# Four elementwise sums of a Conformer encoder's feed-forward blocks moved from VectorE to GpSimd

## The chip, the cores and the metric

The kernel runs on one core of one Trainium2 chip, as one launch. The metric is the device time of one execution in microseconds (us); lower is better. Engines are called by their names or by the profile's short forms: TensorE (PE, with PEld for its weight loads), VectorE (DVE), ScalarE (ACT), GpSimd (POOL) and SyncE (SP), which issues most loads. DMA issues on GpSimd's queue are done by GpSimd itself.

## The reference

Two layers of a Conformer-like block on 512 tokens of 1024 features, in float32:

```python
def swiglu(x, w_gate, w_up, w_down):
    return (jax.nn.silu(x @ w_gate) * (x @ w_up)) @ w_down

for l in range(DEPTH):                       # DEPTH = 2
    x = x + 0.5 * swiglu(rms_norm(x, ffn1_norm[l]), ffn1_w_gate[l], ffn1_w_up[l], ffn1_w_down[l])
    h = rms_norm(x, mix_norm[l])
    p = h @ w_in[l]
    attn = mla_group(...)                    # latent attention, 8 heads
    conv = conv_group(...)                   # gated depthwise convolution
    x = x + jnp.concatenate([attn, conv], axis=-1) @ w_out[l]
    x = x + 0.5 * swiglu(rms_norm(x, ffn2_norm[l]), ffn2_w_gate[l], ffn2_w_up[l], ffn2_w_down[l])
    x = rms_norm(x, post_norm[l])
```

The weights of a feed-forward block are 1024 x 2816 (gate and up) and 2816 x 1024 (down). There are four such blocks, and the change is in these alone.

## The kernel before

**Precision.** Each float32 operand is split into a rounded high part and a low part (operand minus high part), and a product is three matmuls: high x high (L154), high x low (L155), low x high (L156). ScalarE makes the high part of weights (`wh`, L244), VectorE the low part (`wl`, L246, in `split_into`). Where a weight needs no sum, the low part comes from a copy with the sign turned (L389) onto which GpSimd's DMA queue adds the weights from memory (L390, in `subtracted` and `summed`).

**Fewer products.** Most of the feed-forward work uses a Winograd form of Strassen's scheme: a 2 x 2 block product is made with seven block products instead of eight, at the price of sums of the inputs and of the outputs. `pair` makes two of the 22 column blocks of gate and up, from four quarters of the weights, `a11`, `a12`, `a21` and `a22`, which SyncE loads. VectorE makes four sums of these: `s3` (L408), `a21` (L409), `a11` (L410) and last `a12` (L411), each of 128 x 1024. The seven products are, in TensorE's order, `b11` and `b21` (plain quarters), `t2` (weight `a11` after L410), `t3` (weight `s3`), `t1` (weight `a21`), `t4` (plain `a22`) and `b22` (weight `a12` after L411). So the sum of L411 is read only by the last product. Products with 512 columns at a time run through `product_joined` (L373 and L374). Their results are copied or added out of PSUM (L414 to L440), with the activation silu between.

**Output sums.** Of the eleven pairs in a block, the first two are computed plainly, six form two chunks of three, and the last three are plain on the down side. In the six, the results `s` and `s2` of a pair become operands of a down product in the same seven-product form. Their sums are `u` (L449 and L450) and `v` (L451 and L452), each of two halves of 128 x 256. `u` serves the products `t3` and `t2`, `v` the products `t1` and `t4`. `split` (L161 on ScalarE, L162 on VectorE) makes high and low parts of each.

**Down products.** After three pairs, `down` runs twice (two halves of the output columns, `g` 0 and 1) over four weight quarters of 128 x 768, with sums `s3` (L489), `a21` (L491), `a11` (L492) and `a12` (L496). The products are added to `x` (L480, which reads PSUM).

**Order.** A scheduler that simulates a timeline puts each engine's instructions in a fixed order; each engine then works its queue in that order. `after("first")` and the like (`issue_after`) tell it to put instructions behind a named one; this binds only instructions on the named one's own engine. The names here, `"first"`, `"second"`, `"u"` and `"v"`, are all VectorE instructions. Buffers come from pools of a fixed number (four for `fr`, three for `raw`, two for `ls`), so a load can start when the last reader of the old content is done.

**GpSimd elsewhere.** In the feed-forward blocks GpSimd issues the DMAs of L390 and little else. In the mixer stage and around it, it does elementwise work: L144 (low weights of the output projection), L191 (sums of squares), L930 (the convolution) and L173 (powers).

Of the kernel before, what the change touches and what calls it, by code (L numbers as in the profile page):

```python
# [12 lines left out]
ALU = mybir.AluOpType  # L13
# [61 lines left out]
def encoder_kernel(ctx: ExitStack, tc: tile.TileContext, xT, consts, vecs, rgain, wgu1, wd1, wdq1,  # L75
# [21 lines left out]
    def bank():  # L97
        return psum.tile([P, S], FP, tag="ps", name=nm("ps"))
# [4 lines left out]
    V, A, G, T = nc.vector, nc.scalar, nc.gpsimd, nc.tensor  # L103
# [149 lines left out]
    def ffn_body(fpool, l, gx, norm, wgu, wd, wdq, gain, done, w0, halved):  # L253
# [15 lines left out]
        def quarters(w, n, first=False):  # L269

            a = quarter(), quarter() if first else late(), quarter(), quarter()
            for q in range(4):
                nc.sync.dma_start(out=a[q][:, :n], in_=w[q])
            return *a, late()
# [81 lines left out]
        def product(o, w, n, start, stop):  # L356
            with tc.issue_after(order["pe"]):
                for gu in range(2):
                    for k in range(4):
                        hi, lo = X[n][k // 2]  # L360
                        t = slice(k % 2 * HS, (k % 2 + 1) * HS)
                        c = slice(gu * 512 + k * P, gu * 512 + (k + 1) * P)
                        last = mm3(o[:, gu * HS:(gu + 1) * HS], w[0][:, c], w[1][:, c], hi[:, t], lo[:, t],
                                   start and gu == 0 and k == 0, stop and k == 3, True)
            order["pe"] = last
# [16 lines left out]
        def copied(o, src):  # L382
            A.copy(o, src)
            return o
# [15 lines left out]
        def pair(p, quartered):  # L400

            a11, a12, a21, a22, s3 = quarters(wgu[l, p], WC, p == CHUNKS[0][1])
            bx, by, bz = bank(), (bank(), bank()), (bank(), bank())
            product(bx, split_into("a11", a11), "b11", True, True)
            a = copied(tmp(), bx)
            product_joined(by, summed(wgu[l, p, 1], a12), "b21", True)
            with after("first"):
                V.tensor_tensor(s3, a11, a21, ALU.add)  # L408
                V.tensor_tensor(a21, a21, a22, ALU.add)  # L409
                V.tensor_tensor(a11, a11, a21, ALU.add)  # L410
                V.tensor_tensor(a12, a12, a11, ALU.add)  # L411
            s = tmp()
            for c, main, rest in parts(by):
                V.tensor_tensor(a[:, c], a[:, c], main, ALU.add)  # L414
                V.tensor_tensor(a[:, c], a[:, c], rest, ALU.add)
                if c.start == 0:
                    A.activation(s[:, 0:HS], a[:, 0:HS], AF.Silu)
            V.tensor_tensor(s[:, 0:HS], s[:, 0:HS], a[:, HS:S], ALU.mult)
            product(bx, split_into("s2", a11), "t2", False, True)
            r2 = wide(fpool.tile([P, WC], FP, tag="e", name=nm("e"), bufs=1))  # L420
            copied(r2[:, 0], bx)
            product_joined(bz, split_into("s3", s3), "t3", True)
            d = tmp()
            for c, main, rest in parts(bz):
                A.copy(d[:, c], main)
                V.tensor_tensor(d[:, c], d[:, c], rest, ALU.add)  # L426
            product(bx, split_into("s1", a21), "t1", False, True)
            copied(r2[:, 1], bx)
            order["first"] = V.tensor_tensor(r2[:, 1], d, r2[:, 1], ALU.subtract).ins
            product_joined(bz, summed(wgu[l, p, 3], a22), "t4", False)  # L430
            for c, main, rest in parts(bz):
                V.tensor_tensor(r2[:, 0, c], main, r2[:, 0, c], ALU.subtract)
                V.tensor_tensor(r2[:, 0, c], rest, r2[:, 0, c], ALU.add)  # L433
            s2 = tmp()
            s2v = s2.rearrange("p (h t) -> p h t", h=2)
            A.activation(s2v, r2[:, :, 0:HS], AF.Silu)
            V.tensor_tensor(s2v, s2v, r2[:, :, HS:S], ALU.mult)
            product(bx, split_into("s4", a12), "b22", False, True)
            A.activation(s[:, HS:S], bx[:, 0:HS], AF.Silu)
            V.tensor_tensor(s[:, HS:S], s[:, HS:S], bx[:, HS:S], ALU.mult)  # L440
            if not quartered:
                return [split(s), split(s2)]
            h0, h1 = slice(0, HS), slice(HS, S)
            b = slot(FR)
            A.copy(b[:, h0], s[:, h0])
            V.tensor_tensor(b[:, h1], s[:, h0], b[:, h0].bitcast(FP), ALU.subtract)
            b2 = split(s2)
            u, v = fpool.tile([P, S], FP, tag="u", name=nm("u"), bufs=1), tmp()
            V.tensor_tensor(u[:, h0], s[:, h1], s2[:, h1], ALU.subtract)  # L449
            order["u0"] = V.tensor_tensor(u[:, h1], u[:, h0], s[:, h0], ALU.subtract).ins  # L450
            V.tensor_tensor(v[:, h0], s[:, h0], s[:, h1], ALU.subtract)  # L451
            V.tensor_tensor(v[:, h1], s2[:, h0], u[:, h1], ALU.add)  # L452
            us = split(u)
            order["u"] = order["evicted"]
            vs = split(v)
            order["v"], order["vh"] = order["evicted"], order["high"]
            return [{"b11": (b[:, h0], b[:, h1]), "b21": [w[:, h0] for w in b2], "b22": [w[:, h1] for w in b2],
                     "t3": [w[:, h0] for w in us], "t2": [w[:, h1] for w in us],
                     "t1": [w[:, h0] for w in vs], "t4": [w[:, h1] for w in vs]}]

        def down(act, chunk):

            n = 2 * NP * P
            for g in range(2):
                a11, a12, a21, a22, s3 = quarters(wdq[l, g, chunk], n)
                px, py, pz = bank(), bank(), bank()

                def times(o, src, name, start, q=None, lo=None):
                    hi, lo = split_into(name, src, n) if q is None else summed(wdq[l, g, chunk, q], src, n, lo)
                    with tc.issue_after(order["pe"]):  # L470
                        for k in range(NP):
                            for i in range(2):
                                c = slice((i * NP + k) * P, (i * NP + k + 1) * P)
                                last = mm3(o[:, i * HS:(i + 1) * HS], hi[:, c], lo[:, c], *act[k][name],
                                           start and k == 0 and i == 0, k == NP - 1, True)
                    order["pe"] = last

                def add(row, h, o, sign):
                    v = x[:, 4 * g + 2 * (1 - row):4 * g + 2 * (1 - row) + 2, h * HS:(h + 1) * HS]
                    return V.scalar_tensor_tensor(v, o.rearrange("p (m t) -> p m t", m=2), 0.5 * sign, v, ALU.mult,  # L480
                                                  ALU.add).ins
                times(px, a11, "b11", True)
                with after("u0"):
                    add(0, 0, px, 1)
                times(py, a12, "b21", True, 1)
                with after("u"):
                    add(0, 0, py, 1)
                with after("first") if g else nullcontext():
                    V.tensor_tensor(s3[:, :n], a11[:, :n], a21[:, :n], ALU.add)  # L489
                with after("first"):  # L490
                    V.tensor_tensor(a21[:, :n], a21[:, :n], a22[:, :n], ALU.add)  # L491
                    V.tensor_tensor(a11[:, :n], a11[:, :n], a21[:, :n], ALU.add)  # L492
                times(px, a11, "t2", False)
                order["second"] = add(1, 0, px, -1)
                with after("second" if g == 0 else "first"):
                    V.tensor_tensor(a12[:, :n], a12[:, :n], a11[:, :n], ALU.add)  # L496
                lo = subtracted(wdq[l, g, chunk, 3], a22, n)
                with after("u"):
                    times(pz, s3, "t3", True)
                add(1, 1, pz, 1)  # L500
                with after("v"), after("vh"):
                    times(px, a21, "t1", False)
                    order["first"] = add(1, 1, px, -1)
                    times(pz, a22, "t4", False, 3, lo)
                    add(1, 0, pz, 1)
                with after("v"), after("vh"):
                    times(px, a12, "b22", False)
                add(0, 1, px, 1)
# [732 lines left out]
```

## Time and profile before

| | us |
|---|---|
| median of 3 runs | 1804.17 |
| lowest and highest | 1803.3, 1804.97 |
| the profiled execution, its own time | 1804.94 |
| its span, first to last instruction | 1803.1 |

The page of the profile, in part: busy time of each engine (share of the span, count of instructions), the span in 40 slices (a digit is the busy share in tenths), and DMA.

```
DVE  7898988689956989898779989876998668989884
ACT  5565656457953575756645656554779435656564
POOL 1000010258943000000310000002689410000102
PEclk9999999999999999999999999999999999999999
```

The stretches where POOL has a digit of 2 or more are the mixer stages and the ends of blocks; the rows of 0 and 1 are the feed-forward blocks. A row of the timeline has the start in us from the span's start, the duration in us, engine, line, operation, tiles written and read, sizes, and in brackets the engine's idle time before it and what ended that. Records of one engine can overlap a little, since the next instruction starts while the last one drains.

### The profile page before, as it was taken

What the parts mean: (1) busy time and instruction counts of PE and PEld (TensorE: products, weight loads), DVE (VectorE), ACT (ScalarE), POOL (GpSimd) and SP (SyncE); (2) the same over time, 40 slices, a digit from 0 to 9 for tenths busy, and PEclk for the clock granted to TensorE, in tenths of its full rate; (3) what the DMA queues carried; (4) which work ended last, traced back from release to release, by engine and by line L of the source; (5) the groups of instructions that cost most, each with busy time, mean ns of one, the idle gap of its engine ahead of it and who ended that gap; (6) DMA issues with size and microseconds to landing.
All of it is one profiled execution on the core that took longest, in us unless ns stands there. A gap on an engine that the chain in (4) does not pass through costs nothing. (4 is left out here: it accounts for less than half of the span.)

```text
span 1803.1 us, 29267 instructions
## 1 busy us (share of the span) xinstructions
PE 1781.6 (99%) x11334; PEld 1603.1 (89%) x11334; DVE 1493.0 (83%) x2263; ACT 1091.9 (61%) x1721; POOL 420.2 (23%) x343
## 2 busy tenths in 40 slices
PE   9999999999999999999999999999999999999998
PEld 7899999888788899999888999998978788999997
DVE  7898988689956989898779989876998668989884
ACT  5565656457953575756645656554779435656564
POOL 1000010258943000000310000002689410000102
PEclk9999999999999999999999999999999999999999
DMA  5657574325103466665426575743250125575742
GB/s 167 173 127 182 134 174 125 108 88 136 29 24 100 124 167 160 153 159 129 125 63 169 126 191 122 193 110 111 80 151 3 42 83 161 139 183 134 180 119 74
DMA packets 70412, 226.16 MB, mean 125 GB/s; under 512 B 7936, under 2 KB 8320, under 8 KB 70272
## 3 DMA queue, kind: packets, MB, share of 16 engines
q1 hardware_dynamic: 54000, 169.74, 29.7%
q0 software_dynamic: 16128, 54.53, 17.6%
q8 instruction: 89, 1.46, 0.3%
q14 instruction: 51, 0.42, 0.1%
q10 hardware_dynamic: 144, 0.00, 0.0%
HBM read 222.15 MB, written 2.10 MB: 124 GB/s over the span
## 5 line engine op out<-in xcount | busy, mean ns | idle before, releaser
L155 PE MATMUL ps<-r,wh 128*128 128x256 f32 (+1 forms) x2540 | 805.8, 318 | 0.0
L154 PE MATMUL ps<-r,wh 128*128 128x256 f32 (+1 forms) x2540 | 802.9, 320 | 2.3 <-ACT wh L1060 1.5
L156 PE MATMUL ps<-r,wl 128*128 128x256 f32 (+1 forms) x2348 | 750.0, 321 | 1.7 <-DVE wl L246 1.6
L154 PEld LDWEIGHTS ps<-r,wh 128*128 128x128 f32 x2540 | 480.4, 189 | 44.1 <-ACT wh L138 3.7
L155 PEld LDWEIGHTS ps<-r,wh 128*128 128x128 f32 x2540 | 481.4, 190 | 34.2 <-issue 1.4
L156 PEld LDWEIGHTS ps<-r,wl 128*128 128x128 f32 x2348 | 445.0, 190 | 36.7 <-DVE wl L246 3.2
L373 PE MATMUL ps<-xj,wh 128*128 128x512 f32 x864 | 304.8, 392 | 4.6 <-DVE t L426 4.6
L138 ACT CAST wh<-raw 128x1024 fp32r<-128x1024 f32 (+3 forms) x148 | 132.3, 903 | 203.6 <-PE ps L155 100.3
L390 POOL DMA_DIRECT2D ls<-in_wgu x72 | 62.5, 869 | 734.4 <-ACT ls L389 656.5
L244 ACT CAST wh<-fr 128x1024 fp32r<-128x1024 f32 (+1 forms) x160 | 157.8, 986 | 109.7 <-DVE fr L410 51.3
L144 DVE TENSOR_TENSOR wl<-raw,wh 128x1024 fp32r<-128x1024 f32 (+3 forms) x132 | 145.2, 1108 | 84.7 <-ACT wh L138 84.3
L246 DVE TENSOR_TENSOR wl<-fr,wh 128x1024 fp32r<-128x1024 f32 (+1 forms) x160 | 182.1, 1138 | 20.5 <-ACT wh L244 20.5
L373 PEld LDWEIGHTS ps<-xj,wh 128*128 128x128 f32 x864 | 161.3, 188 | 36.3 <-DVE t L426 6.2
L930 POOL TENSOR_TENSOR y<-y,pr 128x511 f32<-128x511 f32 (+14 forms) x120 | 158.1, 1318 | 54.9 <-ACT pr L926 47.5
L374 PE MATMUL ps<-xj,ls 128*128 128x256 f32 x576 | 161.3, 280 | 0.0
L246 DVE TENSOR_TENSOR wl<-raw,wh 128x1024 fp32r<-128x1024 f32 (+1 forms) x100 | 113.4, 1134 | 14.8 <-ACT wh L244 14.4
L244 ACT CAST wh<-raw 128x1024 fp32r<-128x1024 f32 (+1 forms) x100 | 98.1, 981 | 44.7 <-PE ps L155 27.7
L191 POOL TENSOR_TENSOR r<-r,t 128x512 f32<-128x512 f32 x45 | 75.1, 1678 | 175.7 <-ACT t L187 174.9
L374 PEld LDWEIGHTS ps<-xj,ls 128*128 128x128 f32 x576 | 108.3, 188 | 0.2
L389 ACT ACTIVATE ls<-fr 128x1024 fp32r<-128x1024 f32 (+1 forms) x56 | 56.1, 1001 | 85.3 <-PE ps L374 49.5
L926 ACT ACTIVATE pr<-m,vec 128x511 f32<-128x511 f32 (+14 forms) x120 | 85.8, 737 | 12.4 <-POOL y L930 12.4
L922 DVE SCALAR_TENSOR_TENSOR cv<-m,vec,cv 128x511 f32<-128x511 f32 (+14 forms) x120 | 87.8, 732 | 3.6 <-ACT cv L918 2.2
(242 smaller groups left out, 2926.2 us busy)
## 6 DMA issues: line engine op xcount, KB each, us to landing
fr<-in_wgu SPq DMA_DIRECT2D x112, 512.0 KB, 4.2
ls<-in_wgu POOLq DMA_DIRECT2D x72, 512.0 KB, 6.6
raw<-in_wgu SPq DMA_DIRECT2D x62, 512.0 KB, 4.9
fr<-in_wdq SPq DMA_DIRECT2D x48, 384.0 KB, 5.3
ls<-in_wdq POOLq DMA_DIRECT2D x32, 384.0 KB, 4.7
raw<-in_wd SPq DMA_DIRECT2D x32, 384.0 KB, 3.1
raw<-in_wd SPq DMA_DIRECT2D x32, 256.0 KB, 2.7
raw<-in_wcv SPq DMA_DIRECT2D x16, 512.0 KB, 3.6
```

Of the source, the lines that this page charges most:

```text
L138: order["cast"] = A.copy(hi[:, :w], raw[:, :w]).ins
L144: (G if kind in POOLW.split() else V).tensor_tensor(lo[:, :w], raw[:, :w], hi[:, :w].bitcast(FP), ALU.subtract)
L154: T.matmul(o, lh, rh, start=first, stop=False, skip_group_check=free)
L155: T.matmul(o, lh, rl, start=False, stop=False, skip_group_check=free)
L156: order["mm"] = T.matmul(o, ll, rh, start=False, stop=last, skip_group_check=free).ins
L244: A.copy(hi[:, :w], src[:, :w])
L246: order["lo"] = V.tensor_tensor(lo[:, :w], src[:, :w], hi[:, :w].bitcast(FP), ALU.subtract).ins
L373: T.matmul(o, w[0][:, c], both, start=start and k == 0, stop=False, skip_group_check=True)
L374: last = T.matmul(o[:, 0:HS], w[1][:, c], both[:, 0:HS], start=False, stop=k == 3, skip_group_check=True).ins
L922: V.scalar_tensor_tensor(acc[:, s:], u[c][:, :S - s], tap(k), acc[:, s:], ALU.mult, ALU.add)
L926: A.activation(pr[:, s:], u[c][:, :S - s], AF.Copy, scale=tap(k))
L930: order["conv"] = G.tensor_tensor(acc[:, s:], acc[:, s:], pr[:, s:], ALU.add).ins
```

## The change

Four statements name GpSimd (`G`) instead of VectorE (`V`). Operands, sizes and the surrounding `after` blocks stay.

```diff
@@ pair
                 V.tensor_tensor(a11, a11, a21, ALU.add)
-                V.tensor_tensor(a12, a12, a11, ALU.add)
+                G.tensor_tensor(a12, a12, a11, ALU.add)
...
-            V.tensor_tensor(v[:, h0], s[:, h0], s[:, h1], ALU.subtract)
-            V.tensor_tensor(v[:, h1], s2[:, h0], u[:, h1], ALU.add)
+            G.tensor_tensor(v[:, h0], s[:, h0], s[:, h1], ALU.subtract)
+            G.tensor_tensor(v[:, h1], s2[:, h0], u[:, h1], ALU.add)
@@ down
                 with after("second" if g == 0 else "first"):
-                    V.tensor_tensor(a12[:, :n], a12[:, :n], a11[:, :n], ALU.add)
+                    G.tensor_tensor(a12[:, :n], a12[:, :n], a11[:, :n], ALU.add)
```

The built program has 100 instructions fewer on VectorE and 100 more on GpSimd: 36 of L411, 24 each of L451 and L452, and 16 of L496. On GpSimd, L411 stands behind the DMA issues of its own pair and ahead of those of the next; in the third pair of a chunk L496 of the first down half stands ahead of that pair's L451 and L452. The scheduler also moves some neighbours: in the third pair, L418 and the first L426 now stand ahead of the low weights (L246) of the first down product, where they stood behind them, and L491 and L492 of the second down half each stand ahead of an L480 that they stood behind.

## The prediction

> **What bounds the kernel now.** I read the first block of the page, then the busy time by stage, the list of waits, and the timeline of single stretches.
>
> ```profile
> PE 1781.6 (99%) x11334; PEld 1603.1 (89%) x11334; DVE 1493.0 (83%) x2263; ACT 1091.9 (61%) x1721; POOL 420.2 (23%) x343
> ```
>
> TensorE is busy for 1781.6 of 1803.1 us. A change that moves no matrix work can gain what is idle there, about 21 us, and no more; what it can lose is not capped. So the question is whether VectorE (DVE) and GpSimd (POOL) still deliver in time. The change touches stretches that repeat: in each of the four feed-forward blocks there are two chunks of three pairs and two down halves, and then three pairs more. One chunk, and a pair of the last three (columns: stretch, its length, then PE, PEld, DVE, ACT, POOL busy with counts, clock, DMA share, GB/s):
>
> ```profile
> 167.80:188.20 20.40, 20.40 (x151) 19.43 (x151) 16.10 (x25) 13.19 (x19) 1.73 (x2) 1.00 0.68 166
> 188.20:208.00 19.80, 19.80 (x146) 18.79 (x146) 18.95 (x32) 14.43 (x22) 1.73 (x2) 1.00 0.62 146
> 208.00:234.80 26.80, 26.23 (x197) 25.02 (x197) 25.74 (x45) 18.15 (x29) 2.59 (x3) 1.00 0.46 103
> 244.20:258.90 14.70, 14.40 (x120) 14.19 (x119) 13.58 (x16) 8.39 (x10) 1.72 (x2) 1.00 0.75 199
> 279.30:299.10 19.80, 19.80 (x146) 18.82 (x145) 16.89 (x27) 13.44 (x20) 1.73 (x2) 1.00 0.54 128
> ```
>
> TensorE has no gap in four of the five rows as far as records tell, but VectorE has only 0.85 us to spare in the second row and 1.06 in the third: it is nearly a second bound there. GpSimd is almost empty, with nothing but DMA issues (L390). That is the case for the change. What TensorE waited for in all that the change touches:
>
> ```profile
> PE ps L373 <- DVE t L426: 4.6, 8, 0.6
> PE ps L156 <- DVE wl L246: 1.6, 6, 0.3
> ```
>
> Eight waits of 0.57 (one per chunk, in the third row's stretch) and six of about 0.27 (in the fourth's): 6.2 us is all that a lighter VectorE could win.
>
> **The change part by part.** What leaves VectorE:
>
> ```profile
> L411 DVE TENSOR_TENSOR raw<-raw,fr x32: 1215/1216/1220, 97.3 to 1740.8; 128x1024 f32<-128x1024 f32 x32
> L411 DVE TENSOR_TENSOR fr<-fr,fr x4: 1216/1222/1227, 76.5 to 1518.8; 128x1024 f32<-128x1024 f32 x4
> L451 DVE TENSOR_TENSOR t<-t x24: 414/416/419, 98.4 to 1671.4; 128x256 f32<-128x256 f32 x24
> L452 DVE TENSOR_TENSOR t<-t,u x24: 408/415/419, 104.1 to 1672.7; 128x256 f32<-128x256 f32 x24
> L496 DVE TENSOR_TENSOR raw<-raw,fr x16: 941/954/961, 143.9 to 1685.8; 128x768 f32<-128x768 f32 x16
> ```
>
> 100 instructions go; successive VectorE records overlap by some 0.08, so a chunk gets back 3 x 1.13 + 6 x 0.335 + 2 x 0.87 = 7.1 us of VectorE. The order of the built program has the same 100 on GpSimd, so the change does what it says.
>
> What they cost on GpSimd, and on VectorE while they run there, shows in the mixer stage, where GpSimd already adds and subtracts beside VectorE:
>
> ```profile
> 532.37 2.40 POOL L144 TENSOR_TENSOR wl<-raw,wh 128x1024 fp32r<-128x1024 f32 x1 [15.19 <-PE ps L155]
> ...
> 542.08 2.85 POOL L144 TENSOR_TENSOR wl<-raw,wh 128x1024 fp32r<-128x1024 f32 x1
> 544.88 2.29 POOL L191 TENSOR_TENSOR r<-r,t 128x512 f32<-128x512 f32 x1
> ...
> 542.59 0.68 DVE L979 TENSOR_TENSOR x<-x,ps 128x512 f32<-128x512 f32 x1
> 543.19 2.83 DVE L144 TENSOR_TENSOR wl<-raw,wh 128x1024 fp32r<-128x1024 f32 x1
> 545.94 1.78 DVE L168 SCALAR_TENSOR_TENSOR r<-x,vec,r 128x512 fp32r<-128x512 f32 x1
> ...
> 361.80 0.15 DVE L205 TENSOR_SCALAR vtok<-ps 128x4 f32<-128x4 f32 x1
> ...
> 362.04 1.95 POOL L173 TENSOR_TENSOR rtok<-vtok,minus_half 128x4 f32<-128x4 f32 x1 [12.17 <-DVE vtok L205]
> ```
>
> Three things. A free GpSimd sum of 1024 columns takes 2.40. VectorE's L144, two inputs from SBUF and 1.22 by itself, took 2.83 beside GpSimd's L144: GpSimd ended at 544.93, VectorE at 546.02, 1.09 later, so nearly its whole work came after. GpSimd's L191 then ended at 547.17, 1.15 after VectorE's end, and VectorE's next, L168, at 547.72, 0.55 after that. The two take turns, whole instructions at a time; L979, with one input from PSUM, ran its 0.68 inside GpSimd's sum undisturbed. And GpSimd starts 0.09 after the VectorE instruction it waits for (361.95 to 362.04).
>
> So a moved sum doesn't leave the shared resource: it holds off each VectorE instruction with two SBUF inputs, for 1.15 us per 512 columns: 2.3 for L411, 1.72 for L496, 0.58 for L451 or L452, against 1.13, 0.87 and 0.335 on VectorE. Per chunk 6.9 + 3.4 + 3.5 = 13.8 in place of 7.1. The Trainium skill ("SBUF — State Buffer", section "Who interferes with whom") has this as an exclusive lock: an instruction of GpSimd that reads SBUF and one of VectorE with two SBUF inputs block each other for the whole instruction, and whichever issues first has it; the rows above agree on the block. On who comes next where both are queued it leaves room; that is the second rival below.
>
> Where it hurts: the middle pair, times of before.
>
> ```profile
> 186.15 1.21 DVE L410 TENSOR_TENSOR fr<-fr,fr 128x1024 f32<-128x1024 f32 x1
> 187.29 0.41 DVE L440 TENSOR_TENSOR t<-t,ps 128x256 f32<-128x256 f32 x1
> 187.62 0.68 DVE L437 TENSOR_TENSOR t<-t,e 128x512 f32<-128x512 f32 x1
> 188.22 1.22 DVE L411 TENSOR_TENSOR raw<-raw,fr 128x1024 f32<-128x1024 f32 x1
> 189.35 0.42 DVE L451 TENSOR_TENSOR t<-t 128x256 f32<-128x256 f32 x1
> ...
> 190.03 1.22 DVE L246 TENSOR_TENSOR wl<-fr,wh 128x1024 fp32r<-128x1024 f32 x1
> ...
> 191.86 0.28 PE L156 MATMUL ps<-r,wl 128*128 128x256 f32 x1
> ```
>
> L246 makes the low weights of the product t2; it ends at 191.25 and TensorE reads them at 191.86: 0.61 to spare. After the change L410 ends at 187.36, L411 starts on GpSimd at 187.45 and ends at 189.85; L440 (PSUM) runs under it. L437 is held and ends 0.55 later, 190.40. Now GpSimd's turn, L451: 190.98. L449 (held, 256 columns, half of 0.55): 191.26. L246: 1.22 less the overlap: 192.4. TensorE waits 0.53. The third pair (208.04) has the same order and spare. 16 such places: 8.5 us. The first pair of a chunk has no L451 and VectorE idles 4.3 of 20.4 there; the last three pairs have no L451 and 2.9 idle: nothing.
>
> VectorE then lags: 1.15, plus 0.58 for L452, less 0.335. In the middle pair the idle 0.85 and TensorE's own delay take that up. In the third, L426 would be 1.45 late, but in the built order a 0.87 low-weight pass now stands behind its first half instead of ahead: 0.58 late, as much as TensorE. So the old wait of 0.57 stays, and no new one comes.
>
> The end of the third pair, where the down products begin:
>
> ```profile
> 220.73 0.50 PE L373 MATMUL ps<-xj,wh 128*128 128x512 f32 x1 [0.57 <-DVE t L426]
> ...
> 223.88 0.95 DVE L492 TENSOR_TENSOR fr<-fr,fr 128x768 f32<-128x768 f32 x1
> 227.69 0.42 DVE L440 TENSOR_TENSOR t<-t,ps 128x256 f32<-128x256 f32 x1 [0.27 <-ACT t L439]
> 228.49 0.68 DVE L162 TENSOR_TENSOR r<-t,r 128x512 fp32r<-128x512 f32 x1
> 229.77 0.68 DVE L480 SCALAR_TENSOR_TENSOR x<-ps,x 128x512 f32<-128x512 f32 x1
> 231.90 0.94 DVE L246 TENSOR_TENSOR wl<-raw,wh 128x768 fp32r<-128x768 f32 x1
> 234.84 0.94 DVE L496 TENSOR_TENSOR raw<-raw,fr 128x768 f32<-128x768 f32 x1
> ...
> 230.15 0.28 PE L155 MATMUL ps<-r,wh 128*128 128x256 f32 x1
> 233.15 0.28 PE L156 MATMUL ps<-r,wl 128*128 128x256 f32 x1
> ```
>
> The hand-written "after second" binds VectorE's queue alone, so on GpSimd L496 runs as soon as L492 is done (224.83 before), 10 us earlier than it did (234.84), into this dense stretch: 1.72, less the idle 0.27 ahead of L440 that it covers. L451 then comes ahead of L162 (r, read at 230.15, ready at 229.17, spare 0.98): 1.45 + 0.58 - 0.98 = 1.05 of TensorE. L452 runs under the L480, which reads PSUM; with both v sums gone from VectorE the next pass, L246 (ready 232.84, read 233.15), is 2.03 - 0.67 = 1.36 late, against a spare of 0.31 and TensorE's own 1.05: no more. 8 times: 8.4. In the second half L496 leaves the way from L492 to the next low weights, and its wait of 0.3 goes: -2.4 at most, -2 taken.
>
> Queued behind the sums on GpSimd are the DMA issues of L390:
>
> ```profile
> 213.68 0.86 POOL L390 DMA_DIRECT2D ls<-in_wdq  x1 [8.31 <-ACT ls L389]
> ...
> 229.92 0.28 PE L156 MATMUL ps<-r,ls 128*128 128x256 f32 x1
> ```
>
> L452 would end near 214.3, so this one goes 0.6 late; it has over 10 us until its product. Nothing, nor for the SP queue, whose loads follow buffers that TensorE's products free.
>
> Sum: 8.5 + 8.4 - 2 = 14.9 over the profiled execution's own 1804.94 (its span of 1803.1 and 1.8 around it): 1819.8; the median of the three runs, 1804.17, lies 0.8 below it: 1819. A stall early in a chunk may hide part of the next one, so I take 1818. Bounds: no stall but the lost old wait (-2) to VectorE as the bound of both dense stretches, below (+23), and half as much again if the lag runs on into the down halves (+34).
>
> **The rivals.**
> Faster: the turns cost nothing because other spare covers them, and the lighter VectorE removes TensorE's 6.2 us of waits: 1798. It decides if L426's and L246's waits vanish. For it: GpSimd at 23%. Against it: 0.61 of spare against 1.15. Chance 0.13.
> No change: GpSimd loses the race for L451, VectorE taking its queued L449 and L246 first. Then the middle places are 0.58 earlier, 191.8 against 191.86: no stall; the end of the third pair keeps about half: 8.4 / 2 - 2 = 2.2 us, 1806.4. Against it: L191 went ahead of L168 above. Chance 0.14.
> Slower by more: VectorE becomes the bound of the dense stretches. Second row: 18.95 - 1.13 - 0.67 + 2.3 + 1.16 - 0.33 (L440 under) = 20.3 against 19.8; third: 25.74 - 1.13 - 1.34 + 2.3 + 2.32 + 1.72 - 0.33 = 29.3 against 26.8; 3 us per chunk, 24 in all: 1828. For it: idle there is in waits on TensorE that shift with it. Chance 0.16.
>
> **How the numbers follow.** Forecast 0.57, own range 1808 to 1826. About 0.2% (3.6 us) is what a measurement of this kernel tells from no change. Below 1800.6 lies the first rival, 0.13; within, the second, 0.14; above, the rest, 0.73. The range 1800 to 1834 leaves out the first rival's 1798 and the far end of the last one.
>
> **What would show it.** Right: L411 on GpSimd about 2.4; L437 beside it near 2 in place of 0.68; new waits of TensorE on L246 (16 places of 0.5) and on L162; VectorE's busy time not falling by the 79 us of records moved (36 x 1.217 + 48 x 0.415 + 16 x 0.954) but roughly level or higher, as held instructions count as busy; L496 starting right after L492. Wrong: VectorE's records keep their lengths beside GpSimd's sums, or TensorE's waits in the chunks fall.

## Result, and the profile after

| | us |
|---|---|
| before, median of 4 runs | 1803.74 (1802.81 to 1804.97) |
| after, median of 4 runs | 1824.34 (1824.11 to 1825.32) |
| ratio after / before | 1.0115, 95% interval 1.0097 to 1.0132 |

The changed kernel is 20.6 us slower. Its profiled execution took 1824.33 us (span 1822.5), 19.4 more than that of before. The first row of the page:

```profile
PE 1788.6 (98%) x11334; PEld 1603.5 (88%) x11334; DVE 1530.9 (84%) x2163; ACT 1102.6 (60%) x1721; POOL 596.1 (33%) x443
```

VectorE has 100 instructions fewer, 79 us of work by the records of before, and is busy 37.9 us longer (1493.0 to 1530.9). The records of single lines say why. Durations are least / median / most in ns. The first, L437, the change does not touch; the others are the moved sums (four more of L411, on other tiles, take the same 2.41):

```profile
L437 DVE TENSOR_TENSOR t<-t,e x36: 684/2794/2855, 96.5 to 1778.5; 128x512 f32<-128x512 f32 x36
L411 POOL TENSOR_TENSOR raw<-raw,fr x32: 2398/2408/2421, 96.3 to 1759.4; 128x1024 f32<-128x1024 f32 x32
L451 POOL TENSOR_TENSOR t<-t x24: 905/1182/1200, 98.7 to 1688.5; 128x256 f32<-128x256 f32 x24
L452 POOL TENSOR_TENSOR t<-t,u x24: 735/1656/1662, 101.7 to 1690.4; 128x256 f32<-128x256 f32 x24
L496 POOL TENSOR_TENSOR raw<-raw,fr x16: 1848/1996/2070, 135.7 to 1703.2; 128x768 f32<-128x768 f32 x16
```

L437, a product of two SBUF operands that took 0.68 before, now has a median of 2.79: GpSimd's L411 holds it off, and the time it is held counts as busy. Where in the chunk this is paid shows in the busy time by stretch (the second, third and fifth of the prediction's five stretches, at their times of after; PE, PEld, DVE, ACT, POOL):

```profile
189.62:210.17 20.55, 20.18 (x146) 18.84 (x145) 20.39 (x29) 14.79 (x22) 6.96 (x5) 1.00 0.56 142
210.17:236.90 26.73, 25.02 (x181) 23.08 (x180) 26.47 (x38) 17.85 (x28) 10.77 (x9) 1.00 0.46 116
...
282.95:302.74 19.79, 19.79 (x146) 18.82 (x145) 17.81 (x25) 13.56 (x20) 4.16 (x4) 1.00 0.56 128
```

The first row, 19.80 long before, is now 20.55, with VectorE busy for all but 0.16 of it. The last row, a pair of the last three, is 19.79 long and was 19.80: there the moved L411 is free. The end of the middle row lies at another place than before, since L496 has moved, so lengths are better taken from TensorE: a chunk runs from the start of its first L373 to that of what follows.

| | second chunk from, to | its length | eight chunks in all | two of the last three pairs of a block | rest of the span |
|---|---|---|---|---|---|
| before | 169.06, 260.15 | 91.09 | 727.7 | 39.57 | 917.1 |
| after | 171.17, 264.50 | 93.33 | 748.1 | 39.57 | 916.1 |

All of it, 20.4 us, was lost inside the eight chunks, 2.55 in each on average (4.05 in the last). What TensorE waits for there (total, times, longest):

```profile
PE ps L155 <- DVE r L162: 6.7, 8, 0.8
PE ps L156 <- DVE wl L246: 6.0, 16, 0.4
PE ps L373 <- DVE t L426: 4.0, 8, 0.9
PE ps L154 <- DVE x L480: 1.1, 1, 1.1
```

The second row is new: 16 waits at the product t2 of the middle and third pairs. So is the first: 8 waits at the end of the third pair. The old one on L426 shrank a little, and the six old ones on L246 in the second half are gone. The middle pair's timeline shows how the sixteen arise:

```profile
188.26 1.22 DVE L410 TENSOR_TENSOR fr<-fr,fr 128x1024 f32<-128x1024 f32 x1
189.39 0.42 DVE L440 TENSOR_TENSOR t<-t,ps 128x256 f32<-128x256 f32 x1
189.72 2.85 DVE L437 TENSOR_TENSOR t<-t,e 128x512 f32<-128x512 f32 x1
192.61 0.85 DVE L449 TENSOR_TENSOR u<-t,t 128x256 f32<-128x256 f32 x1
193.38 1.21 DVE L246 TENSOR_TENSOR wl<-fr,wh 128x1024 fp32r<-128x1024 f32 x1
...
189.62 2.41 POOL L411 TENSOR_TENSOR raw<-raw,fr 128x1024 f32<-128x1024 f32 x1 [1.96 <-issue]
191.99 1.19 POOL L451 TENSOR_TENSOR t<-t 128x256 f32<-128x256 f32 x1
...
193.77 0.39 PE L154 MATMUL ps<-r,wh 128*128 128x256 f32 x1
193.99 0.28 PE L155 MATMUL ps<-r,wh 128*128 128x256 f32 x1
194.64 0.39 PE L156 MATMUL ps<-r,wl 128*128 128x256 f32 x1 [0.37 <-DVE wl L246]
194.87 0.28 PE L154 MATMUL ps<-r,wh 128*128 128x256 f32 x1
194.98 0.28 PE L155 MATMUL ps<-r,wh 128*128 128x256 f32 x1
```

Read it by ends. L411 ends at 192.03, L437 at 192.57 (0.54 later), L451 at 193.18 (0.61 later), L449 at 193.46 (0.28 later), L246 at 194.59; TensorE takes its weights at 194.64. The two engines alternate by whole instructions. L440, with an operand in PSUM, keeps its 0.42.

Read TensorE by starts. Undisturbed, these matmuls follow each other by 0.12 (194.87 to 194.98). The start at 194.64 came 0.65 after the one before it: 0.53 lost. But the starts on either side (193.77 to 193.99, and 194.64 to 194.87) are also 0.10 too far apart. A stall listed as 0.37 costs 0.73.

The end of the third pair:

```profile
228.03 0.94 DVE L492 TENSOR_TENSOR fr<-fr,fr 128x768 f32<-128x768 f32 x1
229.41 2.27 DVE L437 TENSOR_TENSOR t<-t,e 128x512 f32<-128x512 f32 x1
233.26 1.22 DVE L162 TENSOR_TENSOR r<-t,r 128x512 fp32r<-128x512 f32 x1
...
229.06 2.07 POOL L496 TENSOR_TENSOR raw<-raw,fr 128x768 f32<-128x768 f32 x1
233.03 0.91 POOL L451 TENSOR_TENSOR t<-t 128x256 f32<-128x256 f32 x1 [1.90 <-DVE t L440]
...
233.41 0.28 PE L154 MATMUL ps<-r,wh 128*128 128x256 f32 x1
234.54 0.38 PE L155 MATMUL ps<-r,wh 128*128 128x256 f32 x1 [0.85 <-DVE r L162]
```

L496 starts 0.09 after L492's end, in the dense stretch and not behind the L480 that its `after` block names. It holds L437. Then L451 goes ahead of L162 and holds it, and TensorE starts 1.13 after its last matmul in place of 0.12.

### The profile page after: what moved, and what is told of

Its sections match the earlier page's. It is cut to its first block, busy times and chain, and to the rows that moved or that the text cites. A ratio compares the mean times of both kernels' runs of the same rounds, so it can differ in the third digit from the quotient of the medians.

```text
span 1822.5 us, 29288 instructions
## 1 busy us (share of the span) xinstructions
PE 1788.6 (98%) x11334; PEld 1603.5 (88%) x11334; DVE 1530.9 (84%) x2163; ACT 1102.6 (60%) x1721; POOL 596.1 (33%) x443
## 4 chain that ended last, share of the span: by engine, by line
PE 72%; DVE 17%; ACT 4%; issue 3%; POOL 2%; DMA 1%; SPq 0%; ACTq 0%; DVEq 0%; POOLq 0%
PE ps L154 20%; PE ps L156 19%; PE ps L155 19%; PE ps L373 7%; PE ps L374 4%; DVE t L437 3%; DVE wl L246 3%; POOL y L930 1%; ACT pr L926 1%; ACT r L840 1%; DVE r L162 1%; DVE fr L409 1%; DVE fr L410 1%; PE ps L868 1%; DVE e L433 1%
## 5 line engine op out<-in xcount | busy, mean ns | idle before, releaser
L373 PE MATMUL ps<-xj,wh 128*128 128x512 f32 x864 | 305.5, 392 | 4.0 <-DVE t L426 4.0
L246 DVE TENSOR_TENSOR wl<-fr,wh 128x1024 fp32r<-128x1024 f32 (+1 forms) x160 | 211.3, 1321 | 23.0 <-ACT wh L244 23.0
L373 PEld LDWEIGHTS ps<-xj,wh 128*128 128x128 f32 x864 | 162.5, 188 | 36.5 <-DVE t L426 5.6
L246 DVE TENSOR_TENSOR wl<-raw,wh 128x1024 fp32r<-128x1024 f32 (+1 forms) x100 | 113.0, 1130 | 6.9 <-ACT wh L244 6.2
L411 POOL TENSOR_TENSOR raw<-raw,fr 128x1024 f32<-128x1024 f32 x32 | 77.1, 2408 | 54.7 <-issue 38.5
```

Source lines behind the costliest of these rows:

```text
L246: order["lo"] = V.tensor_tensor(lo[:, :w], src[:, :w], hi[:, :w].bitcast(FP), ALU.subtract).ins
L373: T.matmul(o, w[0][:, c], both, start=start and k == 0, stop=False, skip_group_check=True)
L411: G.tensor_tensor(a12, a12, a11, ALU.add)
```

## The experiments

The theory: GpSimd's sums hold VectorE's instructions with two SBUF operands, turn by turn, and each place where VectorE had under a microsecond to spare becomes a stall of TensorE. The rivals: VectorE is simply full, so that each sum costs by its amount and not by its place; or the wider order of instructions changed, and the sums themselves don't matter; or the sums only come later, and TensorE waits for their results.

**One part at a time.** The sum L411 alone, the output sums L451 and L452 alone, the sum L496 alone, each on GpSimd and all else as before:

```diff
# weight sum of a pair
-                V.tensor_tensor(a12, a12, a11, ALU.add)
+                G.tensor_tensor(a12, a12, a11, ALU.add)
# output sums
-            V.tensor_tensor(v[:, h0], s[:, h0], s[:, h1], ALU.subtract)
-            V.tensor_tensor(v[:, h1], s2[:, h0], u[:, h1], ALU.add)
+            G.tensor_tensor(v[:, h0], s[:, h0], s[:, h1], ALU.subtract)
+            G.tensor_tensor(v[:, h1], s2[:, h0], u[:, h1], ALU.add)
# weight sum of a down half
-                    V.tensor_tensor(a12[:, :n], a12[:, :n], a11[:, :n], ALU.add)
+                    G.tensor_tensor(a12[:, :n], a12[:, :n], a11[:, :n], ALU.add)
```

> Only the last weight sum of each gate/up pair (36 of L411) is on GpSimd; v and the down sum stay on VectorE. Theory (an instruction of GpSimd with SBUF inputs and one of VectorE with two SBUF inputs run in turns): L437 beside it near 2.9 us in place of 0.68, the low weights of t2 (L246) about 1.0 late against 0.61 to spare, a wait of TensorE of 0.4 to 0.5 at 16 places: 1810 to 1813. Rival 1 (nothing is held off, only the results of GpSimd come later): a12 is read by the last product alone, more than 5 us later, so 1803 or a little below. Rival 2 (the new order of the neighbours costs the time): little is reordered here, 1804.

> Only the two v sums of each pair (24 of L451, 24 of L452) are on GpSimd. Theory: each holds the shared access 0.6 us in place of 0.335 on VectorE; 0.25 more at the middle places against 0.61 to spare, and at the end of the third pair 0.6 against 0.98: nothing shows, 1802 to 1806. Rival 1 (late results): v is read by t1 and t4, many us later in the first two pairs; 1803. Rival 2 (the order of L418, L426 and L246 in the third pair, which changes with these): up to 10 above, or below 1803 if it helps.

> Only the last weight sum of each down half (16 of L496) is on GpSimd. Theory: in the first half it runs right after L492 and holds off the dense end of the third pair by 1.72 less 0.27 of idle, against a spare of 0.98 and 0.31: waits of TensorE of 0.5 on L162 and 0.6 on L246, 8 times, 9 us; in the second half the old wait of 0.5 on L246 goes, 4 us: 1807 to 1811. Rival 1 (late results): the sum is done 8 us earlier than before, so no loss, and 1800 with the old wait gone. Rival 2 (order): 1800 to 1804.

| on GpSimd | median us (before 1803.1) | ratio, 95% |
|---|---|---|
| L411 | 1808.59 | 1.0031 (1.0020 to 1.0042) |
| L451 and L452 | 1806.03 | 1.0020 (1.0010 to 1.0030) |
| L496 | 1805.20 | 1.0011 (1.0002 to 1.0021) |

With L411 alone, the record of L437 and the wait on L246:

```profile
L437 DVE TENSOR_TENSOR t<-t,e x36: 684/2796/2867, 96.5 to 1762.2; 128x512 f32<-128x512 f32 x36
PE ps L156 <- DVE wl L246: 3.0, 17, 0.3
PE ps L373 <- DVE t L426: 1.3, 2, 1.1
```

The hold is there in full, and the sixteen places wait. Listed, that is 0.17 at each, but TensorE's starts lose 0.54 at each, 8.7 us in all, a little above the 0.4 to 0.5 expected. The kernel lost only 5.5 us, less than the expected 7 to 10, because old waits shrank beside it: with L411 off VectorE, that on L426 fell from 4.6 us in eight places to 1.3 in two. With the output sums alone, L437 keeps its 0.68, and the cost is elsewhere:

```profile
208.13 1.77 DVE L411 TENSOR_TENSOR raw<-raw,fr 128x1024 f32<-128x1024 f32 x1
212.92 1.65 POOL L452 TENSOR_TENSOR t<-t,u 128x256 f32<-128x256 f32 x1 [4.10 <-DVE u L450]
213.90 1.22 DVE L162 TENSOR_TENSOR r<-t,r 128x512 fp32r<-128x512 f32 x1
PE ps L373 <- DVE t L426: 9.2, 8, 1.9
```

L451 holds L411 (1.77 in place of 1.22). L452 waits for a VectorE instruction's turn (1.65 in place of 0.74 when free), then holds L162 (1.22 in place of 0.68). That is 1.1 of hold for the 0.67 that the two sums took of VectorE, and the wait on L426 doubles from 4.6 to 9.2. In the second chunk L426 still stands behind all that it stood behind before, but for the two sums, so a new order is not the reason. That nothing would show was wrong. With L496 alone the wait on L162 that I expected did not come, and the one on L426 is 4.6 as before; there is a new one, on L480:

```profile
224.83 1.85 POOL L496 TENSOR_TENSOR raw<-raw,fr 128x768 f32<-128x768 f32 x1 [10.52 <-DVE fr L492]
225.63 1.86 DVE L246 TENSOR_TENSOR wl<-fr,wh 128x768 fp32r<-128x768 f32 x1
228.80 0.69 DVE L162 TENSOR_TENSOR r<-t,r 128x512 fp32r<-128x512 f32 x1
PE ps L154 <- DVE x L480: 0.8, 4, 0.2
```

L496 starts early as in the changed kernel, but runs for 0.8 beside VectorE instructions that read PSUM, and then holds L246 for 0.91. Idle time takes up part of that: L162 ends at 229.49, 0.38 ahead of the matmul that reads it (229.87), where it had 0.98. The L480 behind it is what TensorE waits for, listed four times, some 0.5 a chunk by starts. Against this the six old waits on L246 in the second half are gone, and the cost stays below the expected 1807 to 1811.

The parts make 5.5 + 2.9 + 2.1 = 10.5 us; together they cost 20.6. So the cost does not go by amount. The theory says that each part alone draws on spare that, together, can be drawn on only once; the last experiments below look at where.

**GpSimd without the reads.** The four sums replaced by GpSimd instructions of the same size on the same tiles: first memsets, which only write (and wait for no operand, so some run earlier than the sums did), then copies of one operand:

```diff
-                V.tensor_tensor(a12, a12, a11, ALU.add)
+                G.memset(a12, 0.0)          # second kernel: G.tensor_copy(a12, a11)
...
-            V.tensor_tensor(v[:, h0], s[:, h0], s[:, h1], ALU.subtract)
-            V.tensor_tensor(v[:, h1], s2[:, h0], u[:, h1], ALU.add)
+            G.memset(v[:, h0], 0.0)         # second kernel: G.tensor_copy(v[:, h0], s[:, h1])
+            G.memset(v[:, h1], 0.0)         # second kernel: G.tensor_copy(v[:, h1], u[:, h1])
...
-                    V.tensor_tensor(a12[:, :n], a12[:, :n], a11[:, :n], ALU.add)
+                    G.memset(a12[:, :n], 0.0)   # second kernel: G.tensor_copy(a12[:, :n], a11[:, :n])
```

> The four sums are left out: in their places GpSimd sets the same tiles to zero, which reads nothing (so the last weight and v are zero). VectorE is relieved of the same 100 instructions. Theory (turns only where GpSimd reads SBUF): no VectorE record is lengthened, L437 stays at 0.68, TensorE's waits on L246 and L162 do not come, and the old ones on L426 and L246 shrink: 1794 to 1801, below the kernel before. Rival 1 (late results): the same, as nothing is late. Rival 2 (new order of the neighbours, or GpSimd's queue being full and its DMA issues late): 1812 to 1824 as in the changed kernel.

> The four sums are left out: in their places GpSimd copies one of the two inputs (a11 to a12, half of s or u to v), so it reads SBUF once, writes the same tiles, and waits for the same VectorE instructions as in the changed kernel. VectorE is relieved as in the run that only writes (1792). Theory: what counts is that GpSimd reads SBUF; the copies take turns with VectorE's two-input instructions, for as long as a copy lasts (some 1 to 1.2 us for 1024 columns, in place of 2.4), so L437 beside L411's copy at 1.5 to 1.9 in place of 0.68, and a time between 1793 and 1803. Rival (two inputs on GpSimd's side are needed, or it was only the late results): L437 stays at 0.68 and the time at 1792.

Written only: 1792.24 us, ratio 0.9942 (0.9927 to 0.9956). One operand copied: 1792.95 (before 1803.83), ratio 0.9939 (0.9926 to 0.9951). Both are a little faster than expected (1794 to 1801, and 1793 to 1803). Neither has a wait of TensorE on L426, L246 or L162 in its list. Written only:

```profile
L437 DVE TENSOR_TENSOR t<-t,e x36: 682/686/694, 96.2 to 1746.2; 128x512 f32<-128x512 f32 x36
L411 POOL MEMSET raw<- x32: 953/955/956, 90.1 to 1721.0; 128x1024 f32 x32
202.50 1.22 DVE L409 TENSOR_TENSOR fr<-fr,fr 128x1024 f32<-128x1024 f32 x1
203.03 0.65 POOL L451 MEMSET t<- 128x256 f32 x1
```

One operand copied:

```profile
L437 DVE TENSOR_TENSOR t<-t,e x36: 684/1399/1464, 96.2 to 1747.0; 128x512 f32<-128x512 f32 x36
L411 POOL COPY raw<-fr x32: 1040/1042/1052, 96.0 to 1727.9; 128x1024 f32<-128x1024 f32 x32
```

Beside memsets VectorE's sum of two SBUF operands keeps its 1.22, and L437 its 0.69. Beside a copy of 1.04, L437 takes 1.40 (1.5 to 1.9 expected): it is held, but for 0.7 and not 2.1, less than the 1.13 that L411 took of VectorE before. The kernel with memsets has, on TensorE, VectorE and ScalarE, the same instructions in the same order as the changed one, and 100 instructions of GpSimd in place of the sums. So the order did not make the loss; what is left is GpSimd's reads and the time that its sums take: 1824.3 against 1792.2. Nor are late results the cause: in the changed kernel TensorE waits for none of the four sums, and only ScalarE does, for L452, nine times and 3.0 us in all. The Trainium skill ("SBUF — State Buffer", section "Who interferes with whom") says that a VectorE instruction with two SBUF inputs contends with GpSimd where GpSimd reads SBUF, and not where it only writes; the 1.22 beside memsets and the 1.40 beside a copy agree.

A chunk takes 89.48 us with the writes alone (7 of the 8), against a mean of 90.96 before. So TensorE's own work sets 89.48, and a VectorE with 79 us less to do and nothing to hold it would gain some 12 us (8 x 1.48; measured 10.9). That is what the faster rival saw; GpSimd's reads are what stands against it.

**A reorder in place of a move.** The wait on L426 (0.57 a chunk) can be attacked without GpSimd. Before, the low weights of the first down product stood ahead of it in VectorE's queue:

```profile
219.07 0.94 DVE L246 TENSOR_TENSOR wl<-fr,wh 128x768 fp32r<-128x768 f32 x1
219.94 0.41 DVE L418 TENSOR_TENSOR t<-t,t 128x256 f32<-128x256 f32 x1
220.27 0.74 DVE L426 TENSOR_TENSOR t<-t,ps 128x256 f32<-128x256 f32 x2
```

```diff
-                V.tensor_tensor(d[:, c], d[:, c], rest, ALU.add)
+                order["rest"] = V.tensor_tensor(d[:, c], d[:, c], rest, ALU.add).ins
...
-                times(px, a11, "b11", True)
+                with after("rest") if g == 0 else nullcontext(): times(px, a11, "b11", True)
```

> The kernel before, all sums on VectorE, with one order changed: the low weights (L246) of the first down product are put behind the last L426 of the third pair, whose bank TensorE waits for. They had 6.7 us to spare. Theory: the wait of TensorE on L426, 0.7 to 0.85 us counted by the pitch of its matmuls, goes 8 times: 1796 to 1799. Rival: VectorE is full there, so the wait turns up behind, on L432 or at the start of the down products: 1802 to 1804.

1797.34 us (before 1803.83), ratio 0.9965 (0.9951 to 0.9978): this version beats both kernels.

```profile
218.16 0.75 DVE L426 TENSOR_TENSOR t<-t,ps 128x256 f32<-128x256 f32 x2
218.82 0.95 DVE L246 TENSOR_TENSOR wl<-fr,wh 128x768 fp32r<-128x768 f32 x1
PE ps L373 <- DVE t L426: 0.3, 1, 0.3
```

The pair has changed places, seven of the eight waits are gone, and so are the six on L246 in the second half, which was not meant: VectorE reaches L492 of that half earlier, 72.8 into the chunk in place of 74.1. The expected 1796 to 1799 counted L426 alone, so that the number came out is in part luck. The two kernels that follow try to add to it. One puts L496 of the second half alone on GpSimd, the other binds L496 behind the L480 named `"second"` in both halves:

```diff
# second half's sum on GpSimd
-                    V.tensor_tensor(a12[:, :n], a12[:, :n], a11[:, :n], ALU.add)
+                    (G if g else V).tensor_tensor(a12[:, :n], a12[:, :n], a11[:, :n], ALU.add)
# sum behind "second" in both halves
-                with after("second" if g == 0 else "first"):
+                with after("second"):
```

> As the run with L426 first, and the last weight sum (L496) of the second down half alone on GpSimd, where the first run of its own had lost TensorE's wait on L246. Theory: VectorE has 0.87 less to do ahead of that L246, but GpSimd's sum starts after L492, near 244.2, lasts until 246.0, and holds L246 to 246.85 in place of 246.6: the wait of 0.5 stays or grows by 0.2, so 0 to 2 us above the run with L426 first. Rival (no turns): L246 ends 0.6 earlier, the wait goes, 4 us below that run.

> As the run with L426 first, and L496 of the second down half stays on VectorE but is put behind the add of t2 (L480), as in the first half. Theory: L246 starts when ScalarE has the high part, some 0.6 earlier, and TensorE's wait on it (0.5 by the pitch, 8 times) goes: 4 us below the run with L426 first, 1792 to 1795, with nothing moved to GpSimd. Rival: L496 is in the way of a later pass and the wait turns up there: no gain over that run.

The first gives 1798.77, ratio 0.9968 (0.9956 to 0.9981); the second 1797.33, ratio 0.9961 (0.9948 to 0.9973). Neither differs from the reorder alone by more than the runs scatter. In the first, L496 on GpSimd holds the very low weights that it was to make room for:

```profile
241.02 1.86 POOL L496 TENSOR_TENSOR raw<-raw,fr 128x768 f32<-128x768 f32 x1 [1.80 <-DVE fr L492]
242.15 1.55 DVE L246 TENSOR_TENSOR wl<-fr,wh 128x768 fp32r<-128x768 f32 x1
```

L246 takes 1.55 in place of 0.95. The second missed its expected 1792 to 1795: the wait that it was to remove was gone already. L496 does start later (246.82 in the second half, 241.68 without the edit), and a new wait stands behind the second chunk, whose cause no run here shows:

```profile
260.85 0.39 PE L154 MATMUL ps<-r,wh 128*128 128x256 f32 x1 [0.41 <-ACT t L383]
```

**Where the parts stop adding up.** The changed kernel with L496 back on VectorE, and then with L496 of the second half alone on GpSimd:

```diff
# from the changed kernel: L496 back
-                    G.tensor_tensor(a12[:, :n], a12[:, :n], a11[:, :n], ALU.add)
+                    V.tensor_tensor(a12[:, :n], a12[:, :n], a11[:, :n], ALU.add)
# from the changed kernel: first half's back
+                    (G if g else V).tensor_tensor(a12[:, :n], a12[:, :n], a11[:, :n], ALU.add)
```

> The changed kernel with L496 back on VectorE: L411, L451 and L452 are on GpSimd. Theory (one spare per place, used up once): with L411 the middle places have no spare left for L451, so 0.7 at each of 16 places as in the changed kernel, against 0.5 with L411 alone; the end of the third pair keeps its spare of 0.98 against L451's 0.6 and shows no or little wait, where the changed kernel waits 1.4. So 11 to 14 above before, 1815 to 1818, and the early L496 is worth 6 to 9 of the changed kernel's 20.6, not the 2 that it cost alone. Rival (each part costs what it costs alone): 5.5 + 2.9, 1812.

> As the run without L496, but L496 of the second down half on GpSimd too. Theory: as in the run with L426 first, VectorE gets 0.87 back there and is held off about as much: within 2 us of the run without L496. Rival (the second half is where the move helps): 4 us below that run, since TensorE's wait of 0.5 on L246 goes 8 times.

Without L496: 1814.67 (before 1803.34), ratio 1.0064 (1.0047 to 1.0081), no wait on L162. With the second half's: 1817.03, ratio 1.0076 (1.0061 to 1.0091). Without L496:

```profile
PE ps L156 <- DVE wl L246: 6.6, 18, 0.4
```

With the second half's:

```profile
PE ps L156 <- DVE wl L246: 8.6, 20, 0.8
```

L411 with the output sums costs 11.3 us, 1814.67, just under the theory's 1815 to 1818 and above the 1812 of plain addition; the difference to either is within the intervals (the parts alone: 8.4). On top of these, L496 costs 20.6 - 11.3 = 9.3, against 2.1 alone (0.4 to 3.8): here the parts do not add. The second half's L496 makes 2.4 of it, the rest, about 7, is the first half's early L496, which by then meets L451 ahead of L162. The split is of differences of some 2 us between kernels whose chunks vary by up to 1.6 us among themselves (91.69 to 93.33 without L496), so its last microsecond stays open.

The traces show where the parts stop adding up. Here the starts of TensorE's matmuls in the eight chunks of each profiled execution are set against those of the chunk of 89.48 us with the writes alone; the table has by how much they fall behind in each stretch, in us over all eight:

| on GpSimd | t2, both pairs | L426 | end of the third pair | second half | all |
|---|---|---|---|---|---|
| nothing (before) | 0.5 | 6.8 | 0.7 | 3.9 | 11.9 |
| L411 | 8.7 | 4.0 | 2.2 | 1.4 | 16.3 |
| L451 and L452 | 0.0 | 11.2 | 1.0 | 2.0 | 14.2 |
| L496 | 0.5 | 6.6 | 4.9 | 1.1 | 13.1 |
| L411, L451, L452 | 11.9 | 7.2 | 1.0 | 1.5 | 21.6 |
| these and L496 of the second half | 12.1 | 6.7 | 1.0 | 4.5 | 24.3 |
| all four (after) | 12.1 | 5.8 | 12.0 | 2.4 | 32.3 |

Spare that is used only once shows at t2 (8.7 with L411, nothing with L451 alone, 11.9 with both) and above all at the end of the third pair, where L496 adds 4.2 alone and 11.0 on top of the others. The second half shows something else: each part alone wins 1.9 to 2.8 there, out of 3.9 that can be won only once. There L496 is a gain alone (1.1) and a loss on top of L411 and the output sums (1.5 without it, 4.5 with it), though it holds L246 in both (1.86 and 1.79 in the second block, in place of 0.95); why the one costs and the other does not, the runs do not show.

## Why the prediction was right, and where its sum was short

Forecast 1818.0 in 1800 to 1834; measured 1824.34, slower, inside the range and 6.3 above the value. By its steps, for the second chunk, in us of TensorE's starts lost against the usual distance of the same matmuls:

| step | predicted change | before | after | change |
|---|---|---|---|---|
| t2, middle pair | +0.53 | 0 | 0.73 | +0.73 |
| t2, third pair | +0.53 | 0 | 0.74 | +0.74 |
| L426 | 0 | 0.84 | 0.69 | -0.15 |
| end of the third pair | +1.05 | 0 | 1.44 | +1.44 |
| second half | -0.25 | 0.56 | 0 | -0.56 |
| sum | +1.86 | | | +2.20 |

The chunk grew by 93.33 - 91.09 = 2.24.

- **The hold and the turns** were right nearly to the hundredth. From L410's end to L246's the prediction had 5.04, the trace has 194.59 - 189.48 = 5.11; GpSimd started 0.14 after L410 and not 0.09. L451 took its turn ahead of L449 in the middle pair and ahead of L162 at the end, so the no-change rival fell.
- **The terms of the stalls** were mis-sized. The delayed start itself is 0.53 at t2 as predicted and 1.01 at the end (1.05 predicted). What the sum left out is the matmuls around a stall: 0.10 on each side at t2, 0.10, 0.23 and 0.10 at the end. That is 16 x 0.2 + 8 x 0.43 = 6.6 us. Over all eight chunks (the table above) t2 went up by 11.6 where the sum had 8.5, and the end of the third pair by 11.3 where it had 8.4. The trace of before held this: its wait on L426 is listed as 0.57, and its starts lose 0.84.
- **The old waits** on L426 did stay (4.0 against 4.6), as predicted. The second half's wait went, and was worth 0.56 where it stood, not 0.25; over all eight chunks that half lost 1.5 less (2 predicted). But the reason given, L496 leaving VectorE, is not needed for it: with L411 and the output sums moved and L496 still on VectorE, that half had already fallen from 3.9 to 1.5, and the second half's L496 on top raised it to 4.5.
- **"A stall early in a chunk may hide part of the next one"** did not show, and the 1 us taken off for it had no row behind it. The stalls came in full, and the last two chunks are the longest (93.74 and 94.53): one has a wait of 0.9 on L426, the other a single wait of 1.1 on L480, which the prediction did not have.
- **The faster rival** (1798) asked that the waits on L426 and L246 vanish. They did where GpSimd only wrote or read one operand, so its idea of a lighter VectorE was sound and its price was missing. **VectorE as the bound** (1828) came close in time; in the middle pair VectorE is busy 20.39 of 20.55, yet it is so by being held, and TensorE's loss there (0.75) is that of the one place at t2.
- **No cost** was right for the first pair of a chunk and for the last three pairs (39.57 us for two of the latter, before and after) and for the DMA issues behind the sums: no row of TensorE's waits names them.
- **Two readings of the rows of before** were off, without harm to the sum: TensorE is busy throughout in three of the five stretches, not four (26.23 of 26.80 and 14.40 of 14.70 in the others), and the second half's waits are six, 1.6 us as listed, so that "-2.4 at most" counted eight.

## What to carry to other kernels

Before moving a sum to GpSimd, look at which VectorE instructions with two SBUF operands would run beside it, and how much each has to spare until its reader. Here L411 was free in the pairs where VectorE had 2.9 us and more idle, and in the dense ones it held VectorE for 2.1 where it took 1.13 off. An instruction bound behind another by the order of one engine's queue is set free when it moves to another engine, so look where it will run. A reorder within VectorE's queue, which puts what TensorE needs next first, gained 0.35% here, where the move lost 1.15%.

## What the runs showed that I had not expected

A stall of TensorE costs more than the list of waits has: 0.37 listed was 0.73 in starts, since the matmuls on both sides also start 0.22 apart in place of 0.12. A GpSimd copy with a single operand holds VectorE (L437 at 1.40 in place of 0.68), and yet a kernel with 100 such copies is as fast as one with memsets, which hold nothing (1792.95 and 1792.24). And three moves that cost 10.5 us one by one cost 20.6 together, in part because each alone had won the same old wait.
